# A first stage with one level of Strassen's scheme for gate projections, and the softmax division on ScalarE

## The chip, the cores and the metric

The kernel runs on one core of a Trainium2 chip. The metric is the device time of one execution in microseconds. A core has five engines that run side by side: TensorE (PE, matrix products), VectorE (DVE), ScalarE (ACT), GpSimd (POOL) and SyncE (SP, here only a queue of transfers); transfers run on 16 DMA engines.

## What is computed

One step of a decoder layer for 1024 prompt tokens and 8 sample tokens (1032 columns in all), in float32. Cut to what matters here:

```
h = rms_norm(x) * g                                   # 1032 x 1024
rq, rk, rv, rg, sq, sk, sv, sg, mg_r, mg_s = split(h @ w_in)
o_r = rms_norm(retention(rope(rq), rope(rk), rv)) * silu(rg)      # 4 heads, 1024 columns
o_s = sink_attention(rope(norm(sq)), rope(norm(sk)), sv) * silu(sg)   # 16 heads, window 128
merged = sigmoid(mg_r) * (o_r @ w_br_ret) + sigmoid(mg_s) * (o_s @ w_br_swa)
y = x + merged @ w_out
```

`rg` and `sg` are 1024 columns each (8 column tiles of 128), `mg_r` and `mg_s` together 2048 (16 column tiles). The softmax has one extra "sink" term in its denominator.

## The kernel before

Every large product is made of three matmuls on operands split in a high and a low part (`hi*hi + hi*lo + lo*hi`). The splits are made at run time: ACT rounds a copy (`whi`, line 168), POOL or DVE subtracts it (`wlo`, line 169). `h` lies transposed in SBUF for the whole first phase as `hhi` and `hlo`, 8 slices of 128 rows by 1032 tokens.

A *block* is one column tile of `w_in` times one third of the tokens: `gemm_T` (lines 206 to 214), 8 slices of 128 rows by 3 matmuls with 344 moving columns, 24 matmuls that add up in one PSUM bank. Three kinds of gates are blocks: `ret_q` (retention q, line 302), `gate_block` (a SiLU gate, line 279: tanh on ACT, a product on DVE, a product with the attention's output `oT` on POOL, and after the third block a store to `d_o`), and `mg_block` (merge gate, line 292: tanh on ACT, a store to `d_t` from ACT's queue).

The first phase (`groups`, line 695) goes through 8 groups: 4 retention heads (`ret_tile`, line 342, and `ret_rows`), then 4 groups of windowed attention (`swa_tile`, line 492, and `swa_rows`). Each group has 8 token tiles. A tile begins with `gemm_tok`, 24 matmuls with 384 moving columns, and goes on in three to five later parts, which `groups` places between the parts of the tiles behind it (`pipe`). All blocks are filler between them: `FILL[gi]` merge-gate blocks and the 6 gate blocks of the group before (`prev`) are spread over a group's tiles, `TAIL[gi]` of them kept for its last tile. What is left of the merge gates follows behind the last group, together with the last 6 gate blocks. The order written in `groups` gives priorities; the order of the instructions on each engine is planned from them when the kernel is built, by a model of the time line, so that the parts of several steps lie interleaved in an engine's queue.

Weights come in units (`load_unit`, line 151): one transfer into one of 3 `wraw` buffers on SP's queue, then the split into one of `wbufs = 6` pairs. `run_steps` loads up to `look` units ahead.

The step order at the start is: `norm_h` (line 240) for the 9 token tiles, with the loads of the first head's k and v weights, its q weights and the rotary tables in between; the x tiles borrow buffers of the `oT` and `qT` tiles. `softmax_tail` (line 477) ends with the division as one product on DVE, line 490:

```
        nc.vector.reciprocal(out=r[:p, :nh], in_=l[:p, :nh])
        nc.vector.tensor_tensor(out=s[:p], in0=s[:p], in1=r[:p, :nh].unsqueeze(2).broadcast_to([p, nh, P]), op=ALU.mult)
```

Behind the groups `open_a` (line 838) reads the first 7 tiles of the gated retention output back from `d_o` through the two `oT` buffers and splits them (`opA0` to `opA6`, lines 881 and 882) into memory that the windowed attention used. The second phase (`phase23`, line 890) multiplies by `w_br_ret`, `w_br_swa` and `w_out`.

## Time and profile before

| | |
|---|---|
| median of 3 runs | 1188.82 us (1187.67 to 1190.15) |
| the profiled execution: its time, its span | 1189.96 us, 1188.1 us |
| PE busy, PE weight loads busy | 1166.6 us (98%), 1103.2 us (93%) |
| DVE, ACT, POOL busy | 644.3 us (54%), 438.7 us (37%), 429.0 us (36%) |
| mean granted clock of TensorE | 0.997 of full speed |
| PE's share of the chain that ended last | 92% |
| moved by DMA | 116.61 MB, mean 98 GB/s |

Times in the views are microseconds from the first instruction. The duration that is listed for a matmul is longer than the distance to the next one, since matmuls are pipelined; the distance between two starts tells what one costs.

### The profile page before, as it was taken

Reading aid. Unit: us, or ns where it says so; the run is one execution under the profiler, and the core shown is the slowest. Engines: PE = TensorE matmul, PEld = TensorE weight load, DVE = VectorE, ACT = ScalarE, POOL = GpSimd, SP = SyncE. Lnnn points to the kernel's source line nnn. Section 1 sums busy time; section 2 is a strip of 40 time slices with the busy share of each in tenths; the row PEclk is TensorE's granted clock in tenths of the full one; section 3 lists DMA queues with packets and bytes.
Section 4 is the critical chain, followed back from the end, with each engine's and each line's share of the span. In section 5 each row is a group of like instructions: output and inputs, shape, how many; then the busy total and the mean of one; then the engine's idle time right before and its main releaser. Section 6 shows DMA issues by size and latency. Waiting matters only on the chain.

```text
span 1188.1 us, 19187 instructions
## 1 busy us (share of the span) xinstructions
PE 1166.6 (98%) x7116; PEld 1103.2 (93%) x7116; DVE 644.3 (54%) x1798; ACT 438.7 (37%) x1130; POOL 429.0 (36%) x395
## 2 busy tenths in 40 slices
PE   6999999999999999999999999999999999999998
PEld 5899999999989999999999999999999999999876
DVE  5755545544644386776775677477843411654121
ACT  6533333344234235544463446345544210221010
POOL 5325116215325435533563356235751221221010
PEclk9999999999999999999999999999999999999999
DMA  9224114313123411220141014101537744644221
GB/s 321 59 73 115 60 43 146 113 60 94 49 69 84 136 63 46 74 79 7 59 129 43 10 60 126 47 1 37 174 104 242 232 143 138 187 127 142 74 91 69
DMA packets 125165, 116.61 MB, mean 98 GB/s; under 512 B 17480, under 2 KB 113224, under 8 KB 125040
## 3 DMA queue, kind: packets, MB, share of 16 engines
q1 hardware_dynamic: 118160, 106.93, 29.2%
q10 hardware_dynamic: 6912, 8.46, 2.0%
q8 instruction: 56, 0.92, 0.3%
q14 instruction: 37, 0.30, 0.1%
HBM read 84.98 MB, written 32.44 MB: 99 GB/s over the span
## 4 chain that ended last, share of the span: by engine, by line
PE 92%; DMA 2%; DVE 2%; issue 1%; ACT 1%; POOL 1%; SPq 0%; ACTq 0%; POOLq 0%
PE acc L212 16%; PE acc L213 16%; PE acc L214 16%; PE acc L224 10%; PE acc L223 10%; PE acc L222 10%; PE acc L233 1%; PE acc L232 1%; PE sc L532 1%; PE av L441 1%; PE sc L533 1%; PE av L564 1%; PE av L565 1%; PE tr L544 1%; DMA oT<-d_o 1%
## 5 line engine op out<-in xcount | busy, mean ns | idle before, releaser
L169 POOL TENSOR_TENSOR wlo<-wraw,whi 128x1024 fp32r<-128x1024 f32 (+1 forms) x92 | 206.7, 2253 | 311.7 <-ACT whi L168 268.8
L212 PE MATMUL acc<-hhi,whi 128*128 128x344 f32 x864 | 279.9, 324 | 2.0 <-ACT tg L298 2.0
L214 PE MATMUL acc<-hhi,wlo 128*128 128x344 f32 x864 | 277.5, 322 | 0.0
L213 PE MATMUL acc<-hlo,whi 128*128 128x344 f32 x864 | 277.1, 321 | 0.0
L222 PE MATMUL acc<-whi,hhi 128*128 128x384 f32 x512 | 175.6, 344 | 2.3 <-ACT hhi L139 1.2
L224 PE MATMUL acc<-whi,hlo 128*128 128x384 f32 x512 | 175.3, 342 | 0.0
L223 PE MATMUL acc<-wlo,hhi 128*128 128x384 f32 x512 | 175.3, 343 | 0.0
L212 PEld LDWEIGHTS acc<-hhi,whi 128*128 128x128 f32 x864 | 162.9, 188 | 5.5 <-ACT tg L298 2.6
L213 PEld LDWEIGHTS acc<-hlo,whi 128*128 128x128 f32 x864 | 162.6, 188 | 1.6
L214 PEld LDWEIGHTS acc<-hhi,wlo 128*128 128x128 f32 x864 | 162.6, 188 | 1.6 <-issue 0.4
L168 ACT ACTIVATE whi<-wraw 128x1024 fp32r<-128x1024 f32 (+1 forms) x92 | 90.4, 984 | 177.3 <-PE acc L213 114.3
L147 POOL TENSOR_TENSOR rs<-ms,nhalf 128x1 f32<-128x1 f32 (+3 forms) x81 | 69.4, 858 | 216.7 <-DVE ms L146 192.4
L222 PEld LDWEIGHTS acc<-whi,hhi 128*128 128x128 f32 x512 | 97.5, 191 | 6.1 <-issue 2.5
L224 PEld LDWEIGHTS acc<-whi,hlo 128*128 128x128 f32 x512 | 97.3, 190 | 0.5 <-DVE hlo L140 0.2
L223 PEld LDWEIGHTS acc<-wlo,hhi 128*128 128x128 f32 x512 | 97.4, 190 | 0.4
L288 POOL TENSOR_TENSOR oT<-oT,tg 128x344 f32<-128x344 f32 x48 | 48.3, 1007 | 63.1 <-DVE tg L286 58.6
L486 ACT ACTIVATE s<-sc,ng,rs 128x128 f32<-128x128 f32 x128 | 57.0, 456 | 17.4 <-DVE ng L483 17.3
L224 PE MATMUL acc<-whi,mlo 128*128 128x512 f32 x128 | 50.5, 395 | 0.0
L223 PE MATMUL acc<-wlo,mhi 128*128 128x512 f32 x128 | 50.3, 393 | 0.0
L222 PE MATMUL acc<-whi,mhi 128*128 128x512 f32 x128 | 50.1, 393 | 0.0
L965 DVE TENSOR_TENSOR x<-acc,x 128x512 f32<-128x512 f32 x16 | 11.0, 690 | 68.7 <-PE acc L224 68.7
L286 DVE SCALAR_TENSOR_TENSOR tg<-tg,acc 128x344 f32<-128x344 f32 x48 | 24.5, 511 | 35.7 <-ACT tg L285 35.5
(357 smaller groups left out, 2394.8 us busy)
## 6 DMA issues: line engine op xcount, KB each, us to landing
wraw<-in_w_in SPq DMA_DIRECT2D x36, 512.0 KB
d_t<-tg ACTq DMA_DIRECT2D x48, 172.0 KB
d_o<-oT SPq DMA_DIRECT2D x16, 516.0 KB
tt<-d_t SPq DMA_DIRECT2D x48, 172.0 KB
wraw<-in_w_in SPq DMA_DIRECT2D x32, 256.0 KB
st<-d_o SPq DMA_DIRECT2D x9, 516.0 KB
d_m<-tt SPq DMA_DIRECT2D x24, 172.0 KB
mm<-d_m SPq DMA_DIRECT2D x24, 172.0 KB
```

Source lines behind the costliest of these rows:

```text
L147: nc.gpsimd.tensor_tensor(out=rs[:p, :width], in0=ms[:p, :width], in1=self.nhalf[:p, :width], op=ALU.pow)
L168: nc.scalar.activation(out=hi[:, :f], in_=raw[:, :f], func=AF.Copy)
L169: nc.gpsimd.tensor_tensor(out=lo[:, :f], in0=raw[:, :f], in1=hi[:, :f].bitcast(F32), op=ALU.subtract)
L212: nc.tensor.matmul(ps, whi[:, k, :], hi[:, cs], start=(k == 0), stop=False)
L213: nc.tensor.matmul(ps, whi[:, k, :], lo[:, cs], start=False, stop=False)
L214: nc.tensor.matmul(ps, wlo[:, k, :], hi[:, cs], start=False, stop=(k == KT - 1))
L222: nc.tensor.matmul(ps, hi[:, k, a:b], whi[:, kk, :], start=(k == 0), stop=False)
L223: nc.tensor.matmul(ps, hi[:, k, a:b], wlo[:, kk, :], start=False, stop=False)
L224: nc.tensor.matmul(ps, lo[:, k, a:b], whi[:, kk, :], start=False, stop=(k == KT - 1))
L286: nc.vector.scalar_tensor_tensor(out=tg[:], in0=tg[:], scalar=1.0, in1=ps[:, :BL], op0=ALU.add, op1=ALU.mult)
L288: nc.gpsimd.tensor_tensor(out=sl, in0=sl, in1=tg[:], op=ALU.mult)
L486: nc.scalar.activation(out=s[:p, j, :], in_=src[j], func=AF.Exp, bias=ng[:p, j : j + 1], scale=scale[j], accum_out=l[:p, j : j + 1])
```

## The change

**Strassen's scheme.** A new first stage, `phase0`, stands ahead of the groups. It takes `norm_h` (with buffers of its own), computes the merge gates of the first 4 column tiles as blocks as before, builds sums of parts of `h` on POOL, DVE and ACT (`make_T`, for two quarters q of the tokens), and then computes 3 pairs of merge-gate column tiles and all 8 retention-gate column tiles (4 pairs) in a 2 by 2 split: the 1024 rows of the inner dimension in two halves, the two column tiles, and the tokens in two halves. A pair takes 7 products (`product`) for each of two quarters q: 4 slices of 128 rows by 3 matmuls with 258 moving columns. The weight operands of a pair are made by `load_part`: two loads, four sums on DVE, three and a half splits. ACT and DVE combine the products (`keep`, `put`). Merge gates go to `d_t`, retention gates to a new DRAM tensor `d_g`; later `gate_apply` reads them back and multiplies `oT` by them on POOL where a `gate_block` stood.

**The groups** lose this filler: `FILL` and `TAIL` become shorter, the retention groups keep only their own `ret_q` blocks, and the first head's k, v and q weights and the tables are loaded behind `phase0`.

**The softmax division** becomes four activations on ACT with a scale for each partition.

```
 RAW = 3
 NA1 = 7
-XQ = 4
 XPOOL = (6,)
-QAT = (1, 2, 4)
+HALF = TOK // 2
+QT = HALF // 2
+B11, B21, B22, T1, T3, T4, T2 = range(7)
+FIRST = 4
+PAIRS = 3
 ROW = [2, 0, 0, 0, 2, 0, 0, 1]
-FILL = [3, 2, 2, 2, 9, 9, 9, 4]
-TAIL = [2, 4, 4, 5, 3, 5, 5, 2]
+FILL = [0, 0, 0, 0, 7, 3, 3, 1]
+TAIL = [0, 0, 0, 0, 1, 1, 1, 0]
...
+def pair_units(col):
+    return [("S", col, part) for part in range(4)]
...
+        if spec[0] == "S":
+            return self.load_part(*spec[1:])
...
+    def load_part(self, col, part):
+        nc = self.nc
+        if part == 0:
+            self.praw = []
+            for e in range(2):
+                raw = self.t(self.wp, [P, D], "wraw", bufs=RAW)
+                src = self.i["w_in"][0, :, col + e * P : col + (e + 1) * P].rearrange("(k p) c -> p k c", p=P)
+                nc.sync.dma_start(out=raw[:].rearrange("p (k c) -> p k c", k=KT), in_=src)
+                self.praw.append(raw)
+        one, two = self.praw
+        if part == 1:
+            self.sums = self.t(self.sp, [P, 3, 512], "wsum", bufs=1)
+            s1, s2, s4 = [self.sums[:, k] for k in range(3)]
+            a11, a12, a21, a22 = one[:, 0:512], one[:, 512:1024], two[:, 0:512], two[:, 512:1024]
+            nc.vector.tensor_tensor(out=s1, in0=a21, in1=a22, op=ALU.add)
+            nc.vector.tensor_tensor(out=s2, in0=s1, in1=a11, op=ALU.subtract)
+            nc.vector.tensor_tensor(out=s4, in0=a12, in1=s2, op=ALU.subtract)
+            nc.vector.tensor_tensor(out=a21, in0=a11, in1=a21, op=ALU.subtract)
...
+        if part == 2:
+            self.nsd += 1
+            both = self.sd[:, self.nsd % 2 * 1024 : (self.nsd % 2 + 1) * 1024]
+            hi, lo = both[:, :512], both[:, 512:]
+        else:
+            hi = self.t(self.wp, [P, D], "whi", F32R, bufs=self.wbufs)[:]
+            lo = self.t(self.wp, [P, D], "wlo", F32R, bufs=self.wbufs)[:]
+        nc.scalar.activation(out=hi, in_=src, func=AF.Copy)
+        nc.gpsimd.tensor_tensor(out=lo, in0=src, in1=hi.bitcast(F32), op=ALU.subtract)
+        return hi, lo
...
+        small = lambda u: u[0] == "S" and u[2] == 2
+
+        def room(idx):
+            kind = small(units[len(loaded)])
+            n = sum(1 for j in range(len(loaded)) if last[j] >= idx and small(units[j]) == kind)
+            return n < (2 if kind else self.wbufs)
...
+    def operand(self, q, b, j, x):
+        c = q * QT + (HALF if b == B22 else 0)
+        if b >= T1:
+            return self.T[q][j][x][:, b - T1, :]
+        h = (self.hhi, self.hlo)[x]
+        return h[:, j + (4 if b != B11 else 0), c : c + QT]
+
+    def product(self, ps, part, half, q, b, start=True, stop=True, **kw):
+        nc = self.nc
+        whi, wlo = part
+        for j in range(4):
+            ws = slice(half * 512 + j * P, half * 512 + (j + 1) * P)
+            hi, lo = [self.operand(q, b, j, x) for x in range(2)]
+            nc.tensor.matmul(ps[:, :QT], whi[:, ws], hi, start=(start and j == 0), stop=False, **kw)
+            nc.tensor.matmul(ps[:, :QT], whi[:, ws], lo, start=False, stop=False, **kw)
+            nc.tensor.matmul(ps[:, :QT], wlo[:, ws], hi, start=False, stop=(stop and j == 3), **kw)
+
+    def ring(self):
+        self.ncc += 1
+        return self.cc[:, self.ncc % 4 * HALF : (self.ncc % 4 + 1) * HALF].rearrange("p (h n) -> p h n", h=2)
...
+    def pair_steps(self, col, q, finish):
+        nc = self.nc
...
+        def put(e, half, a, b, op=ALU.add):
+            if e not in v:
+                v[e] = self.ring()
+            nc.vector.tensor_tensor(out=v[e][:, half], in0=a[:, :QT], in1=b, op=op)
+
+        def keep(name, of):
+            v[name] = self.t(self.gp, [P, BL], "tg", bufs=3)[:, :QT]
+            nc.scalar.activation(out=v[name], in_=v[of][:, :QT], func=AF.Copy)
+
+        def p1(us):
+            self.product(acc("X"), us[0], 0, q, B11, True, False, **part)
+            keep("s1", "X")
+
+        def p2(us):
+            self.product(acc("Y"), us[0], 1, q, B21)
+            put(0, 0, v["Y"], v["s1"])
+
+        def p5(us):
+            self.product(acc("Z"), us[0], 0, q, T1, True, False, **part)
+            keep("s5", "Z")
+
+        def p6(us):
+            self.product(v["X"], us[0], 1, q, T2, False, False, **part)
+            keep("s2", "X")
+
+        def p3(us):
+            self.product(v["Z"], us[0], 0, q, B22, False, True, **part)
+            put(0, 1, v["Z"], v["s2"])
+            finish(0, q, v[0])
+
+        def p4(us):
+            self.product(acc("W"), us[0], 1, q, T4)
+            keep("s4", "W")
+
+        def p7(us):
+            self.product(v["X"], us[0], 0, q, T3, False, True, **part)
+            put(1, 1, v["X"], v["s5"])
+            put(1, 0, v["X"], v["s4"], ALU.subtract)
+            finish(1, q, v[1])
+
+        a, m, d, b = pair_units(col)
+        return [([a], p1), ([a], p2), ([m], p5), ([m], p6), ([d], p3), ([b], p4), ([b], p7)]
...
+    def make_T(self, q, pool, scratch):
+        nc = self.nc
+        self.T[q] = []
+        h0 = slice(q * QT, (q + 1) * QT)
+        h1 = slice(HALF + q * QT, HALF + (q + 1) * QT)
+        H, L = self.hhi[:].bitcast(F32), self.hlo[:].bitcast(F32)
+        for j in range(4):
+            r = scratch(j)[:, : 4 * QT].rearrange("p (a n) -> p a n", a=4)
+            left = lambda x: x[:, j::4, h1]
+            right = lambda x: x[:, j].rearrange("p (h n) -> p h n", h=2)[:, :, h0]
+            nc.gpsimd.tensor_tensor(out=r[:, 0:2], in0=left(H), in1=right(H), op=ALU.subtract)
+            nc.gpsimd.tensor_tensor(out=r[:, 2:4], in0=left(L), in1=right(L), op=ALU.subtract)
+            nc.vector.tensor_tensor(out=r[:, 0:2], in0=r[:, 0:2], in1=r[:, 2:4], op=ALU.add)
+            nc.vector.tensor_tensor(out=r[:, 3], in0=H[:, j + 4, h1], in1=r[:, 0], op=ALU.subtract)
+            nc.vector.tensor_tensor(out=r[:, 3], in0=r[:, 3], in1=L[:, j + 4, h1], op=ALU.add)
+            nc.gpsimd.tensor_tensor(out=r[:, 2], in0=r[:, 3], in1=H[:, j + 4, h0], op=ALU.subtract)
+            nc.gpsimd.tensor_tensor(out=r[:, 2], in0=r[:, 2], in1=L[:, j + 4, h0], op=ALU.subtract)
+            hi, lo = [self.t(pool, [P, 4, QT], f"T{q}{j}{x}", F32R) for x in "hl"]
+            nc.scalar.activation(out=hi[:], in_=r, func=AF.Copy)
+            nc.vector.tensor_tensor(out=lo[:], in0=r, in1=hi[:].bitcast(F32), op=ALU.subtract)
+            self.T[q].append((hi, lo))
...
+    def put_quarter(self, dst, src, q):
+        self.nc.scalar.dma_start(out=dst.rearrange("p (h q n) -> p q h n", h=2, q=2)[:, q], in_=src)
+
+    def mg_pair(self, c, q, cc):
+        self.nc.scalar.activation(out=cc, in_=cc, func=AF.Tanh, scale=0.5)
+        self.put_quarter(self.d_t[c], cc, q)
+
+    def gate_pair(self, kt, q, cc):
+        nc = self.nc
+        tg = self.ring()
+        nc.scalar.activation(out=tg, in_=cc, func=AF.Tanh, scale=0.5)
+        nc.vector.scalar_tensor_tensor(out=tg, in0=tg, scalar=1.0, in1=cc, op0=ALU.add, op1=ALU.mult)
+        self.put_quarter(self.d_g[kt], tg, q)
+
+    def gate_apply(self, kt, nb, oT, i):
+        nc = self.nc
+        n0 = nb * BL
+        tg = self.t(self.gp, [P, BL], "tg", bufs=3)
+        nc.sync.dma_start(out=tg[:], in_=self.d_g[kt][:, n0 : n0 + BL])
+        sl = oT[:, i, n0 : n0 + BL]
+        nc.gpsimd.tensor_tensor(out=sl, in0=sl, in1=tg[:], op=ALU.mult)
+        if nb == NB - 1:
+            self.stored = nc.sync.dma_start(out=self.d_o[kt], in_=oT[:, i, :])
+
+    def phase0(self):
+        nc, tc = self.nc, self.tc
...
+        def begin(us):
+            self.sp = enter("sp")
+            ctx["pT0"] = enter("T0"), ctx["T0"]
+            self.xb = enter("xb")
+
+        def t0(us):
+            pool = ctx.pop("pT0")[0]
+            self.make_T(0, pool, lambda j: self.t(self.xb, [P, 4 * QT], "scr", bufs=2))
+
+        def t1(us):
+            leave("xb")
+            pool = enter("T1")
+            raw = [self.t(self.gp, [P, 2, TOK], "oT", bufs=2)[:].rearrange("p a b -> p (a b)") for _ in range(2)]
+            self.make_T(1, pool, lambda j: raw[j % 2][:, j // 2 * 1032 :])
+            self.sd = self.t(self.gp, [P, 2, TOK], "oT", F32R, bufs=2)[:].rearrange("p a b -> p (a b)")
+            self.cc = self.t(self.gp, [P, 2, TOK], "oT", bufs=2)[:].rearrange("p a b -> p (a b)")
+            self.nsd = self.ncc = 0
+
+        def end(us):
+            for name in ("T1", "T0", "sp"):
+                leave(name)
+
+        x = lambda t: ([], lambda us: self.norm_h(t), 0)
+        w = lambda u: ([u], nop, 0)
+        first = [tch(OFF_MR + c * P) for c in range(FIRST)]
+        conv = lambda nb: [([u], (lambda us, c=c, nb=nb: self.mg_block(us[0], c, nb)), 4 if nb == 2 else 0) for c, u in enumerate(first)]
+        steps = [([], begin, 0), x(0), w(first[0]), x(1), w(first[1]), x(2), w(first[2]), x(3), w(first[3])]
+        steps += [x(t) for t in range(4, NT + 1)]
+        steps += conv(0) + [([], t0, 0)] + conv(1) + [([], t1, 0)] + conv(2)
+        jobs = [(OFF_MR + c * P, lambda e, q, cc, c=c: self.mg_pair(c + e, q, cc)) for c in range(FIRST, FIRST + 2 * PAIRS, 2)]
+        jobs += [(OFF_RG + c * P, lambda e, q, cc, c=c: self.gate_pair(c + e, q, cc)) for c in range(0, KT, 2)]
+        for col, fin in jobs:
+            for q in range(2):
+                steps += self.pair_steps(col, q, fin)
+        steps.append(([], end))
+        steps.append(([tch(OFF_RQ)], nop))
+        self.run_steps(steps, 4)
...
         nc = self.nc
         p = P if t < NT else NS
         cs = slice(t * P, t * P + p)
-        if t == XQ:
-            x = self.t(self.ap, [P, TOK], "qT", bufs=2)[:, :D]
-        else:
-            i = t - (t > XQ)
-            if i % 2 == 0:
-                self.xpair = self.t(self.gp, [P, 2, TOK], "oT", bufs=2)
-            x = self.xpair[:, i % 2, :D]
+        x = self.t(self.xb, [P, D], "xt", bufs=4)
         nc.sync.dma_start(out=x[:p], in_=self.i["x_prompt"][0, cs, :] if t < NT else self.i["x_sample"][:, 0, :])
         if t == 0:
-            self.gb = self.t(self.ap, [P, D], "st", bufs=1)
+            self.gb = self.t(self.xb, [P, D], "gb")
...
-        nc.vector.tensor_tensor(out=s[:p], in0=s[:p], in1=r[:p, :nh].unsqueeze(2).broadcast_to([p, nh, P]), op=ALU.mult)
+        for j in range(nh):
+            nc.scalar.activation(out=s[:p, j, :], in_=s[:p, j, :], func=AF.Copy, scale=r[:p, j : j + 1])
...
+            with tc.tile_pool(name="pacc0", bufs=6, space=PSUM, reuse_waits="tile") as self.pacc, \
+                    tc.tile_pool(name="ptr0", bufs=2, space=PSUM, reuse_waits="tile") as self.ptr:
+                self.phase0()
...
-        mg = [([tch(OFF_MR + c * P)], (lambda us, c=c, nb=nb: self.mg_block(us[0], c, nb))) for c in range(16) for nb in range(NB)]
+        mg = [([tch(OFF_MR + c * P)], (lambda us, c=c, nb=nb: self.mg_block(us[0], c, nb))) for c in range(FIRST + 2 * PAIRS, 16) for nb in range(NB)]
...
-                col = (OFF_RG + kt * P) if gi < 4 else (OFF_SG + (kt - 8) * P)
+                col = OFF_SG + (kt - 8) * P
                 for nb in range(NB):
+                    if gi < 4:
+                        yield ([], (lambda us, kt=kt, nb=nb, i=i: self.gate_apply(kt, nb, st["o"], i)))
+                        continue
...
-        x = lambda t: ([], lambda us: self.norm_h(t), 0)
-        w = lambda u: ([u], nop, 0)
-        steps += [([], begin, 0), x(0), w(kv[0]), x(1), w(kv[1]), x(2), w(kv[2]), w(kv[3]), ([], tables, 0), x(3), w(qu),
-                  x(4), x(5), rope_block(0), x(6), x(7), x(8), rope_block(1), rope_block(2)]
+        steps += [([], begin, 0), rope_block(0), ([], tables, 0), rope_block(1), rope_block(2)]
...
-                if h:
-                    put(*qs)
+                put(*qs)
...
-                if gi == 0 and t in QAT:
-                    put(qs[QAT.index(t)])
```

## Rows read from the trace of the kernel before

**Rows 1.** The page, part 1: busy time, share of the span, instructions.
```profile
PE 1166.6 (98%) x7116; PEld 1103.2 (93%) x7116; DVE 644.3 (54%) x1798; ACT 438.7 (37%) x1130; POOL 429.0 (36%) x395
```

**Rows 2.** Stretches of the start: length, busy time of each engine, clock, DMA.
```profile
28.00:32.00 4.00, 4.00 (x17) 4.00 (x17) 3.12 (x16) 3.59 (x9) 0.73 (x2) 0.61 1.14 303
...
sum 60.00, PE 46.47 PEld 42.94 DVE 40.14 ACT 34.33 POOL 27.10; mean PE 3.10 PEld 2.86 DVE 2.68 ACT 2.29 POOL 1.81
```

**Rows 3.** PE's instructions in order of time, the start.
```profile
11.20 0.69 PE L222 MATMUL acc<-whi,hhi 128*128 128x384 f32 x1 [1.19 <-ACT hhi L139]
...
20.51 0.60 PE L271 MATMUL tr<-ident,oT 128*128 128x128 f32 x4
```

**Rows 4.** PE's instructions in order of time: start, duration, line, tile, shapes.
```profile
66.08 0.32 PE L214 MATMUL acc<-hhi,wlo 128*128 128x344 f32 x1
...
67.96 0.32 PE L214 MATMUL acc<-hhi,wlo 128*128 128x344 f32 x1
...
71.46 0.28 PE L202 MATMUL sc<-Shi,qhi 128*128 128x256 f32 x1
...
72.17 0.38 PE L339 MATMUL tr<-ident,on 128*128 128x128 f32 x2
```

**Rows 5.** Groups by line, PE's weight loads: busy, mean ns, idle before.
```profile
L213 PEld LDWEIGHTS acc<-hlo,whi 128*128 128x128 f32 x864 | 162.6, 188 | 1.6
```

**Rows 6.** Stretches of the groups: busy PE, PEld, DVE, ACT, POOL, clock, DMA.
```profile
310.00:360.00 50.00, 50.00 (x309) 45.47 (x309) 26.19 (x95) 20.09 (x60) 10.28 (x14) 1.00 0.19 58
760.00:830.00 70.00, 70.00 (x438) 65.79 (x437) 54.32 (x186) 32.04 (x98) 25.64 (x27) 1.00 0.06 19
421.00:833.00 412.00, 411.84 (x2577) 392.21 (x2576) 288.78 (x940) 192.55 (x571) 188.49 (x182) 1.00 0.18 55
...
833.00:905.00 72.00, 70.57 (x453) 69.29 (x452) 43.70 (x82) 34.52 (x80) 40.59 (x36) 1.00 0.51 164
60.00:390.00 330.00, 330.00 (x2083) 312.95 (x2082) 167.28 (x507) 126.75 (x337) 112.63 (x115) 1.00 0.27 84
```

**Rows 7.** The same stretches, line 212 alone (8 of its matmuls a block).
```profile
310.00:360.00 50.00, 5.39 (x16) 3.00 (x16) 1.00 0.19 58
760.00:830.00 70.00, 18.11 (x56) 10.52 (x56) 1.00 0.06 19
...
833.00:905.00 72.00, 41.01 (x128) 23.93 (x128) 1.00 0.51 164
```

**Rows 8.** Groups by line and shape: the division on DVE.
```profile
L490 DVE TENSOR_TENSOR s<-s,r 128x512 f32<-128x512 f32 x32 | 23.1, 721 | 0.6
```

**Rows 9.** Groups by line and shape: ACT with a scale for each partition.
```profile
L354 ACT ACTIVATE khi<-kr,misc 128x128 fp32r<-128x128 f32 x32 | 12.8, 399 | 16.0 <-DVE kr L322 11.5 <-PE av L203 4.5
```

**Rows 10.** Groups by line and shape: POOL's products and differences.
```profile
L169 POOL TENSOR_TENSOR wlo<-wraw,whi 128x1024 fp32r<-128x1024 f32 x60 | 145.2, 2422 | 284.1 <-ACT whi L168 241.2 <-PE acc L233 42.8
...
L288 POOL TENSOR_TENSOR oT<-oT,tg 128x344 f32<-128x344 f32 x48 | 48.3, 1007 | 63.1 <-DVE tg L286 58.6 <-DVE mx L539 4.0 <-DVE l L488 0.5
```

**Rows 11.** PE and DVE in order of time, from retention to windowed attention.
```profile
396.92 0.39 PE L369 MATMUL av<-qT,kT 128*128 128x128 f32 x2
...
414.31 0.75 DVE L455 TENSOR_TENSOR qr<-acc,Aswa_q_g 128x256 f32<-128x256 f32 x2 [3.03 <-POOL Aswa_q_g L649]
...
417.01 0.44 PE L222 MATMUL acc<-whi,hhi 128*128 128x384 f32 x1 [1.15 <-DVE tg L286]
```

**Rows 12.** DVE in order of time, and the chain of waits, 820 to 925.
```profile
884.08 0.85 DVE L571 TENSOR_TENSOR oT<-av,rbig 64x256 f32<-64x256 f32 x2 [7.90 <-ACT rbig L567]
...
900.40 6.18 DMA oT<-d_o
...
907.80 1.30 DVE opA6l L882
```

More of the change, by code (lines that the diff above doesn't have):

```diff
@@ L186, in run_steps @@
         loaded = [self.loaded[u] for u in pre]
-        def live(idx):
-            return sum(1 for j in range(len(loaded)) if last[j] >= idx)
+        small = lambda u: u[0] == "S" and u[2] == 2
[3 more added lines that the diff above has]
+            return n < (2 if kind else self.wbufs)
         for idx, (us, fn, look) in enumerate(steps):
             top = max([max(n) for n in need[: idx + 1] if n], default=-1)
-            while len(loaded) < len(units) and len(loaded) <= top + look and live(idx) < self.wbufs:
+            while len(loaded) < len(units) and len(loaded) <= top + look and room(idx):
                 loaded.append(self.load_unit(units[len(loaded)]))
@@ L669, in build @@
             self.d_t = [self.t(dp, [P, TOK], f"d_t{k}") for k in range(16)]
+            self.d_g = [self.t(dp, [P, TOK], f"d_g{k}") for k in range(8)]
             self.d_m = [self.t(dp, [P, TOK], f"d_m{k}") for k in range(8)]
@@ L727, in first @@
             return (us, fn), ([], more)
-        kv = slabs([(OFF_RK, DK), (OFF_RV, DV)])
-        qu = tch(OFF_RQ)
         def begin(us):
```

24 lines of the change are left out of this document (23 added, 1 removed).

## The prediction

> **What bounds the kernel now.** I read the page first: PE is busy for 1166.6 of 1188.1 us, and no other engine comes over 54% [rows 1]. A number of PE instructions, times what each costs, is therefore the first measure of this change; the second is whether PE still finds work wherever filler is taken away. For the second I read stretches. In the first 60 us PE loses 13.5 us, and part of the rest runs at half clock (0.61 of full speed in one row, which is a mix of the 1.2 and 2.4 GHz levels) [rows 2]. From 60 to 390 (retention) and from 421 to 833 (windowed attention) it loses 0.0 and 0.2 us; from 833 to 905, where the attention ends and `open_a` reads back, 1.4 us [rows 6]. The reader is to see that filler makes PE full: in the windowed attention DVE is at 70% of the stretch, and from 760 to 830 blocks are 38% of PE's time [rows 6, 7].
>
> **What a block costs, and a product.** The listed durations overlap, so I count starts. Twelve matmuls of 344 columns go from 66.08 to 67.96, 0.1567 us each; six of 256 columns from 71.46 to 72.17, 0.1183 us each [rows 4]. A block is 24 x 0.1567 = 3.76 us. The line through the two gives 0.1192 us for 258 columns. A pair of column tiles was 6 blocks, 144 matmuls, 22.56 us; it becomes 2 x 7 x 12 = 168 matmuls, 20.03 us. That is 2.53 us less, not an eighth, because there are more matmuls and each has a part that does not shrink with its columns. Seven pairs: **-17.7 us**. At the price of 256 columns it would be -18.8.
>
> The price of 168 matmuls at no less than the old pitch is a rival below. It comes from the Trainium skill's page "Perfetto Trace Analysis", section "Identifying the Most-Contended Engine", which judges TensorE's headroom by the busy share of its weight loads and not of its matmuls. By that, loads at 93% [rows 1] would make 24 more weight loads a pair a loss. The trace disagrees so far: a load lasts 188 ns, yet starts of 256-column matmuls, each with a load of its own, lie 118 ns apart [rows 4, 5].
>
> **The start, 0 us.** Transposes of the first tile still wait for x. Before, products began at 11.20; a block needs three token tiles, and the third tile's second half is transposed at 20.51 [rows 3], so about 9 us of half-clock work moves back. In return the tables (five transfers) are no longer on SP's queue among the x tiles, x has four buffers, and the later waits of the 13.5 us find 12 blocks (45 us) that need nothing else. I take 0, between -4 and +4.
>
> **Making the sums of h, +1 us.** Per slice POOL has two operations of 516 elements and two of 258. Between 1.007 us for 344 and 2.422 us for 1024 [rows 10] that is 1.37 and 0.83, so 4.4 us a slice, 35 us for eight. The blocks run from about 20 to 70 us. POOL can begin near 31 us, when the seventh tile is split, is done near 66, and still needs 2.4 us for the first pair's low part. It just fits. Late by a whole quarter's sums it would cost 10: bounds 0 and 10.
>
> **The pairs, +1 us.** In 20 us a pair asks POOL for 3 x 2.4 + 1.2 = 8.5 us and DVE and ACT for about 10 each, so they hide. Between the fifth product and the third, ACT must copy Z out while PE does one product (1.43 us); behind a 1 us weight split it is late. I allow 0.07 us for each of 14 quarters; bounds 0 and 4.
>
> **Into retention, +1 us.** Rotary tables and slabs now load at the end of `phase0`. Three `ret_q` blocks (11.3 us) cover what is late; without them all of it would stall: 0 to 8.
>
> **The thinner retention groups, +1 us.** 27 blocks go (3 + 3 x 8), 102 us of the stage. From 60 to 390, 330 us become some 228 with DVE at 167 at most (73%) and ACT at 127 (56%) [rows 6]. Blocks will be the three `ret_q` in 57 us, 20%. The nearest row is 310 to 360: two blocks (16 matmuls of line 212, 15% of PE) and PE at 50.00 of 50 [rows 6, 7]. So dense, at bounds 0 and 10. `gate_apply` adds 24 loads to SP's queue; each waits for one of three `tg` buffers, that is for POOL's product, and behind it stand weight loads. Three raw buffers and six split pairs loaded ahead hide it; else a unit comes late by the product's 1.0 us [rows 10].
>
> **Into the windowed attention, +2 us.** Between the last retention score at 396.92 and the first rotary product at 414.31 the new group has no tables; PE lives on two gemms and blocks and loses 1.15 us at 417.01 [rows 11]. Then 9 and 6 blocks were at hand; now 7, without gates. Bounds 0 and 10.
>
> **The body, with the division, +1 us.** 8 + 6 + 6 + 3 = 23 blocks go, 86.5 us, so 412 become 325. DVE gives up 32 x 0.721 = 23.1 us [rows 8] and is left with 266 (82%). ACT takes 128 activations; the nearest row, of 128x128 with a scale for each partition, is 0.399 us [rows 9], so 51 us more, 244 at most (75%). Both stay below PE. The nearest row is 760 to 830: seven blocks, 38% of PE, DVE at 78%, PE at 70.00 of 70 [rows 6, 7]. Groups with 9 blocks are like it; the two with 7 are thinner. Chain per tile: 0.72 us becomes up to 4 x 0.40. Bounds 0 and 8.
>
> **The end of the attention, +4 us.** From the last product on `oT` at 884.08 to `opA6` at 909.1 runs a chain of its own, 25 us: gates, store, loads (one takes 6.18 us), splits [rows 12]. From 833 to 905, 128 / 8 = 16 blocks covered it and the last tiles [rows 7]; now 6 gates and 4 merge-gate blocks do, 22.6 us less. DVE is busy for 43.7 of these 72 us [rows 6], so the last tiles can finish earlier once PE is free for them, which gives most back. Bounds 0 and 22.6; I take 4, nearer the lower.
>
> **Sum.** -17.7 + 0 + 1 + 1 + 1 + 1 + 2 + 1 + 4 = -6.7 us on the profiled execution's 1189.96, which lies 1.1 us above the median: 1182 us. The likeliest case reaches from 1176 to 1186. 0.2% (2.4 us) is what a measurement can tell from no change.
>
> **Rivals.**
> Dense everywhere: the planner packs the thinner stages as well as before (for it: zero idle at 15% filler; against it: PE already slips where filler is short, 833 to 905). The small terms fall to 2: 1189.96 - 1.1 - 15.7 = 1173. Chance 0.27.
> The tail starves, slower than before: the last tiles take as long as now and the chain into `opA6` finds no block left. The full 22.6 us stand for the 4: 1201. It decides from 11 us of idle there. For it: that chain is already the last to end. Against it: DVE's slack. Chance 0.20.
> DVE and ACT become the bound in the thin attention groups: at half of the upper ends, entry and body cost 9 us in place of 3, 1188, no gain. For it: 82% and 75%. Against it: 78% beside a full PE. Chance 0.10.
> Weight loads bind, so that Strassen doesn't do what it says: 168 x 0.1567 = 26.3 us a pair, +3.8 each, +26 for -17.7: 1226. Against it the 118 ns. Chance 0.03.
> The forecast has 0.40. Faster: 0.38 + 0.27 + 0.02 = 0.67; same 0.11; slower 0.22. The range takes in the dense case with the start's gain (1168) and almost all of the tail's case: 1168 to 1199.
>
> **What would show it.** Starts 0.119 us apart in the pairs, a pair in 20 us. PE without waits from 25 to 65, and no wait for POOL where the first product on sums begins. PE idle under 1 us in each retention group. In the attention groups waits of PE on DVE or ACT of a few us. Behind the last tile, waits on `opA` splits of 5 to 7 us. I am wrong if the pitch is above 0.125 (the pairs' gain is gone at 0.134), if PE waits for over 10 us behind the last tile, or if retention shows 10 us of idle.

## The result and the profile after

The changed kernel takes 1257.89 us (median of 4, 1256.78 to 1260.19) beside 1188.24 of the kernel before on the same chip: a ratio of 1.0586, 95% interval 1.0566 to 1.0607. It is slower by 69.7 us, where 6.7 us of gain were forecast; the range ended at 1199.

The page after, part 1, as [rows 1]:

```profile
PE 1175.2 (94%) x7284; PEld 1096.2 (87%) x7284; DVE 718.6 (57%) x1870; ACT 510.2 (41%) x1326; POOL 489.4 (39%) x441
```

PE's idle time grew from 21.5 us (1188.1 less 1166.6) to 79.9 (1255.1 less 1175.2). Its busy time grew by 8.6 us although the products became 17.7 us cheaper, and the mean granted clock fell from 0.997 to 0.979. The granted clock was 0.50, the lower level of 1.2 GHz, for 52 us in all. PE was busy for 33.3 of them and idle for the others (the sum over these stretches):

```profile
sum 51.99, PE 33.34 PEld 29.08 DVE 35.60 ACT 20.32 POOL 24.77; mean PE 4.17 PEld 3.64 DVE 4.45 ACT 2.54 POOL 3.10
```

So half of 33.3, 16.7 us of PE's busy time, is lost to the clock, against 3.4 before; what else is lost at the lower level is idle time and counted there. Where PE loses its time, the stretches after tell (length, busy time of each engine with its instructions, clock, DMA), in the form of [rows 2, 6]:

```profile
0.00:60.00 60.00, 41.76 (x254) 39.42 (x255) 37.35 (x49) 31.14 (x54) 34.08 (x31) 1.00 0.56 169
60.00:120.00 60.00, 48.90 (x325) 47.40 (x324) 39.32 (x45) 22.78 (x37) 44.94 (x32) 0.83 0.19 62
120.00:240.00 120.00, 120.00 (x994) 119.83 (x993) 51.07 (x80) 51.28 (x93) 52.30 (x27) 1.00 0.37 115
240.00:510.00 270.00, 266.78 (x1661) 247.13 (x1660) 176.39 (x534) 111.46 (x326) 97.53 (x111) 1.00 0.33 105
510.00:540.00 30.00, 18.61 (x106) 16.08 (x105) 12.54 (x54) 6.14 (x19) 16.68 (x21) 0.79 0.47 148
540.00:930.00 390.00, 361.19 (x2151) 331.90 (x2150) 286.82 (x912) 215.24 (x674) 176.51 (x183) 0.98 0.17 51
930.00:990.00 60.00, 56.55 (x344) 53.88 (x343) 27.63 (x56) 32.28 (x74) 22.77 (x22) 0.97 0.35 119
```

The pairs (120 to 240) and retention (240 to 510) are full, as forecast. Three places are not: the making of the sums (60 to 120), the entry to windowed attention (510 to 540) and its body (540 to 930). With the idle time, and half of the time in which PE was busy at the lower clock (5.6, 2.3 and 7.1 us), they lose 17, 14 and 36 us.

**The pairs.** These two starts are 15 matmuls apart: 0.1193 us each, so a pair of 168 matmuls takes 20.0 us, as predicted.

```profile
179.96 0.28 PE L279 MATMUL acc<-T03h,whi 128*128 128x258 f32 x1
...
181.75 0.28 PE L279 MATMUL acc<-hhi,oT 128*128 128x258 f32 x1
```

**The sums of h.** POOL's instructions in order of time (start, duration, in brackets the idle time before and what ended it):

```profile
48.21 2.56 POOL L349 TENSOR_TENSOR scr<-hhi 128x516 f32<-128x516 f32 x2 [6.15 <-ACT hhi L146]
...
59.34 6.93 POOL L349 TENSOR_TENSOR oT<-hhi 128x516 f32<-128x516 f32 x4 [0.18 <-ACT hhi L146]
66.22 1.32 POOL L349 TENSOR_TENSOR scr<-hhi 128x516 f32<-128x516 f32 x1
...
90.47 0.64 POOL L354 TENSOR_TENSOR scr<-scr,hhi 128x258 f32<-128x258 f32 x1 [0.89 <-DVE scr L353]
```

It begins at 48, not 31, and the second quarter's sums (`oT`) run ahead of the first quarter's third and fourth slice (`scr`), which are done only past 90. PE waits for them (its longest wait from 60 to 120: total, times, longest). During the wait its clock falls to the lower level, and it stays there while PE works in pieces:

```profile
PE acc L279 <- ACT T02h L357: 7.9, 1, 7.9
```

```profile
84.00:88.00 4.00, 1.01 (x9) 0.81 (x7) 3.96 (x7) 0.00 (x0) 2.54 (x3) 0.86 0.00 0
88.00:92.00 4.00, 0.00 (x0) 0.00 (x0) 2.26 (x4) 0.17 (x1) 2.69 (x5) 0.50 0.00 0
92.00:96.00 4.00, 2.67 (x9) 2.08 (x9) 1.23 (x1) 0.91 (x2) 3.95 (x5) 0.50 0.00 0
...
104.00:108.00 4.00, 4.00 (x22) 4.00 (x22) 3.49 (x7) 2.67 (x4) 1.17 (x2) 0.58 0.01 4
```

**The entry.** POOL stands on `gate_apply` (line 381), whose loads are late, before it makes the attention's tables (lines 864 to 867); PE's first rotary transpose waits 11.16 us. In [rows 11] the longest wait of PE is 1.15, before another instruction:

```profile
519.68 1.81 POOL L381 TENSOR_TENSOR oT<-oT,tg 128x344 f32<-128x344 f32 x2 [5.72 <-DMA tg<-d_g]
...
533.26 0.78 POOL L866 TENSOR_TENSOR Bswa_q_g<-s,gbn 128x288 f32<-128x288 f32 x1
```

```profile
535.22 0.66 PE L727 MATMUL tr<-ident,qr 128*128 128x128 f32 x2 [11.16 <-DVE qr L684]
```

**The body.** These are the longest waits from 540 to 930, by engine. PE's are many and short: 19.4 of 28.8 us for an accumulator, 7.5 for the probabilities that POOL masks. The longest of ACT and DVE are for each other:

```profile
PE acc L443 <- DVE tg L501: 6.9, 5, 2.2
PE acc L262 <- DVE tg L501: 5.5, 4, 2.2
PE av L781 <- POOL pLp L769: 3.8, 4, 1.6
PE av L780 <- POOL pHp L769: 3.4, 3, 2.0
```

```profile
ACT s L701 <- DVE ng L698: 35.9, 17, 4.3
ACT qs L732 <- DVE qs L733: 30.7, 22, 2.9
```

```profile
DVE l L703 <- ACT ds L702: 27.7, 20, 2.2
```

Such waits alone are no sign of loss. Over the whole stage of the windowed attention, from the first rotary transpose to the last product with v, DVE's longest wait in total is the same before, when PE was full, and after:

```profile
DVE l L488 <- ACT ds L487: 32.0, 22, 2.8
```

```profile
DVE l L703 <- ACT ds L702: 32.1, 23, 2.2
```

DVE is busy for 74% of the stretch from 540 to 930 and ACT for 55%. Neither is full, and yet the stage is shorter by much less than the blocks that it lost. From the first rotary transpose to the last product with v (535.22 to 968.41; before 421.34 to 882.86), first the whole row, and under it line 262 (before 212) alone, 8 of whose matmuls make a block:

```profile
535.22:968.41 433.19, 403.12 (x2400) 369.91 (x2400) 307.12 (x981) 238.71 (x742) 196.03 (x203) 0.98 0.18 53
...
535.22:968.41 433.19, 106.91 (x320) 62.33 (x320) 0.98 0.18 53
```

The same two of before:

```profile
421.34:882.86 461.52, 459.93 (x2886) 439.10 (x2885) 321.44 (x1011) 216.89 (x636) 221.44 (x214) 1.00 0.21 62
...
421.34:882.86 461.52, 155.94 (x482) 90.64 (x482) 1.00 0.21 62
```

60.25 blocks became 40: 20.25 x 3.76 = 76 us of PE's work left the stage, which got only 28.3 us shorter. It lost 48 us.

### The profile page after: what moved, and what is told of

Its sections match the earlier page's. It is cut to its first block, busy times and chain, and to the rows that moved or that the text cites. A ratio compares the mean times of both kernels' runs of the same rounds, so it can differ in the third digit from the quotient of the medians.

```text
span 1255.1 us, 20010 instructions
## 1 busy us (share of the span) xinstructions
PE 1175.2 (94%) x7284; PEld 1096.2 (87%) x7284; DVE 718.6 (57%) x1870; ACT 510.2 (41%) x1326; POOL 489.4 (39%) x441
## 5 line engine op out<-in xcount | busy, mean ns | idle before, releaser
L178 POOL TENSOR_TENSOR wlo<-wraw,whi 128x1024 fp32r<-128x1024 f32 (+1 forms) x78 | 171.2, 2203 | 248.2 <-ACT whi L177 166.4
L262 PE MATMUL acc<-hhi,whi 128*128 128x344 f32 x528 | 174.1, 332 | 9.2 <-DVE tg L501 6.2
L264 PE MATMUL acc<-hhi,wlo 128*128 128x344 f32 x528 | 172.4, 327 | 0.0
L263 PE MATMUL acc<-hlo,whi 128*128 128x344 f32 x528 | 172.3, 326 | 0.0
L177 ACT ACTIVATE whi<-wraw 128x1024 fp32r<-128x1024 f32 (+1 forms) x78 | 75.2, 969 | 114.0 <-PE acc L453 43.6
L262 PEld LDWEIGHTS acc<-hhi,whi 128*128 128x128 f32 x528 | 101.8, 193 | 12.8 <-DVE tg L501 7.5
L263 PEld LDWEIGHTS acc<-hlo,whi 128*128 128x128 f32 x528 | 101.6, 192 | 0.8
L264 PEld LDWEIGHTS acc<-hhi,wlo 128*128 128x128 f32 x528 | 101.3, 192 | 0.6
L299 DVE TENSOR_TENSOR oT<-acc,tg 128x258 f32<-128x258 f32 x56 | 22.4, 421 | 59.7 <-PE acc L281 57.3
L215 POOL TENSOR_TENSOR wlo<-wraw,whi 128x1024 fp32r<-128x1024 f32 x14 | 36.0, 2574 | 38.0 <-ACT whi L214 38.0
```

The costliest lines, as they stand in the source:

```text
L177: nc.scalar.activation(out=hi[:, :f], in_=raw[:, :f], func=AF.Copy)
L178: nc.gpsimd.tensor_tensor(out=lo[:, :f], in0=raw[:, :f], in1=hi[:, :f].bitcast(F32), op=ALU.subtract)
L215: nc.gpsimd.tensor_tensor(out=lo, in0=src, in1=hi.bitcast(F32), op=ALU.subtract)
L262: nc.tensor.matmul(ps, whi[:, k, :], hi[:, cs], start=(k == 0), stop=False)
L263: nc.tensor.matmul(ps, whi[:, k, :], lo[:, cs], start=False, stop=False)
L264: nc.tensor.matmul(ps, wlo[:, k, :], hi[:, cs], start=False, stop=(k == KT - 1))
```

## Experiments

Three theories stand at the start. A, thin filler: the blocks that went to the new stage were PE's cover for the attention's chains. B: the division on ACT lengthens these chains. C: the new stage costs more than its products save.

The kernel before ran beside each group of runs; its median lies between 1187.98 and 1189.17 us. A difference between runs of different groups is therefore good to 1 or 2 us.

### Which part of the change costs the time

**The division back on VectorE**, in the changed kernel:

```
-        for j in range(nh):
-            nc.scalar.activation(out=s[:p, j, :], in_=s[:p, j, :], func=AF.Copy, scale=r[:p, j : j + 1])
+        nc.vector.tensor_tensor(out=s[:p], in0=s[:p], in1=r[:p, :nh].unsqueeze(2).broadcast_to([p, nh, P]), op=ALU.mult)
```

> The changed kernel with one part undone: the softmax division is again one VectorE instruction per tile. Three theories. A, thin filler: the merge-gate blocks that went to the new stage were TensorE's cover for the chains of the windowed attention; without them it waits. B, the division: four ScalarE activations behind the reciprocal lengthen each tile's chain and hold up ScalarE's queue. C, the new stage itself: the sums of h and what stands around them cost what the products save and more. A and C: the division is a small part, 1245 to 1262 us. B: the attention's loss goes, 1225 us or less.

1248.15 us, ratio to before 1.0489 (1.0471 to 1.0507): by the medians the division is 9.7 of the 69.7 us, by the ratios 11.5.

**The division alone**, the reverse edit in the kernel before.

> The kernel before with the softmax division alone moved to ScalarE. A and C: with all its filler the attention hides the longer chain, 1184 to 1196 us. B: 1210 us or more.

1194.94 us, 1.0042 (1.0030 to 1.0054): 5.8 us with all the filler. B is a part and not the main cause.

**Plain blocks in the pairs' place**, no sums:

```
-        for col, fin in jobs:
-            for q in range(2):
-                steps += self.pair_steps(col, q, fin)
+        steps += [([tch(OFF_MR + c * P)], lambda us, c=c, nb=nb: self.mg_block(us[0], c, nb)) for c in range(FIRST, FIRST + 2 * PAIRS) for nb in range(NB)]
+        steps += [([tch(OFF_RG + c * P)], lambda us, c=c, nb=nb: self.gate_early(us[0], c, nb)) for c in range(KT) for nb in range(NB)]
```

> The changed kernel with the seven pairs computed by 42 plain blocks at the same place ahead of retention, and no sums of h or of weights. The order of everything behind the stage is the same. A: the products cost 17.7 us more, the sums' stall of about 15 us goes, the attention is as thin as in the changed kernel: about 1260 us, 1245 to 1272. C: the loss goes with the sums, 1215 us or less.

1254.31 us, 1.0540 (1.0521 to 1.0559). Without any Strassen product the loss is the same but for 3.6 us: it lies in what was moved, and in the division, which this run keeps. The stage as built costs as much as its products save.

**The filler given back**:

```
-PAIRS = 3
-FILL = [0, 0, 0, 0, 7, 3, 3, 1]
-TAIL = [0, 0, 0, 0, 1, 1, 1, 0]
+PAIRS = 0
+FILL = [0, 0, 0, 0, 10, 9, 9, 4]
+TAIL = [0, 0, 0, 0, 3, 5, 5, 2]
```

> The changed kernel with pairs for the retention gates alone (four in place of seven); the six merge-gate columns of the other three pairs are plain blocks again and stand in the attention groups, 10, 9, 9 and 4 merge-gate blocks with 4 left behind the last group, held back as before the change. A: three pairs' gain is lost (+7.6), some 25 to 35 of the attention's 41 us come back and most of the 12 at its entry: about 1222 us, 1210 to 1238. B and C: nothing comes back, 1258 to 1270.

1225.83 us, 1.0301 (1.0282 to 1.0320): 32 us faster with three pairs' gain given up. The body is dense again (4.6 us idle in its whole stage); the wait at the entry is still 11.6 us.

**The kernel before, thinned**: nothing but merge-gate blocks moved to retention, 23 from the attention groups and 2 from behind them (the 18 of the expectation are miscounted; in the stage, blocks fall from 60.3 to 40.8). The blocks kept for each last tile become as few as in the changed kernel.

```
-FILL = [3, 2, 2, 2, 9, 9, 9, 4]
-TAIL = [2, 4, 4, 5, 3, 5, 5, 2]
+FILL = [8, 8, 8, 10, 1, 3, 3, 1]
+TAIL = [2, 4, 4, 5, 1, 1, 1, 0]
```

> The kernel before with nothing changed but where its plain blocks stand: 18 merge-gate blocks of the attention groups go to the retention groups (8, 8, 8, 10 and 1, 3, 3, 1), held back as in the changed kernel, so that each attention group has as many blocks as there. No sums, no pairs, the division on VectorE. If thin filler alone makes the attention wait, 1218 to 1242 us. If the new stage or the division were needed for it: 1195 us or less.

1240.90 us, 1.0444 (1.0429 to 1.0460). The same 7116 instructions on PE, in another order, cost 52 us more. A is shown, in the kernel before, with no part of the change in it. 19.5 blocks, 73 us, left the stage, which got 25.5 us shorter (436.0 for 461.5): 48 us lost, as in the changed kernel. Part 1 of its page:

```profile
PE 1184.5 (95%) x7116; PEld 1112.7 (90%) x7116; DVE 675.7 (54%) x1798; ACT 434.9 (35%) x1130; POOL 428.5 (35%) x395
```

Against [rows 1], 34.9 us of idle time and 17.9 us of busy time are added. Of the latter 12.6 are the clock (0.985 for 0.997 on the mean): PE was busy for 32 us at 0.50, before for 6.8.

### The sums of h and the entry

The first four start from the kernel with the filler given back (1225.83 us).

**Gate products later at the entry**: `k = 8 if gi == 4 else 2` blocks stand ahead of `prev` in a group.

> The kernel of the run with the filler given back (four pairs, 1225.8 us), and in the first attention group the six gate products on GpSimd go behind eight merge-gate blocks in place of two. That run still waits 11.6 us where the first rotary product needs the attention's tables: GpSimd stands on the gate products, whose loads are late, ahead of the tables it has to make, and TensorE has no block to do. If that order is the cause, 8 to 12 us come back: 1213 to 1219 us. Rival: the tables' loads behind the change of pools are late by themselves: 1223 to 1228 us.

1225.03 us. The time is in the rival's range, but not for the rival's reason: the wait falls from 11.6 to 5.4 us, so the order does matter there. PE's idle time falls by 3.1 us in all (57.5 to 54.4) and the time hardly; in the rest of the stage PE idles 3.4 us more. That blocks used at the entry are missing later would explain it, and was not tried by itself.

**Four scratch slices**: `make_T(0, ...)` gets the two `oT` tiles that `make_T(1, ...)` uses behind it.

> The same kernel of 1225.8 us, and the sums of the first quarter get four scratch slices (the two oT tiles that the second quarter uses behind them) in place of a ring of two, so that GpSimd no longer turns to the second quarter before the first is done. If the ring of two is what makes the first quarter late, 8 to 14 of the 16 us that the stage loses come back: 1211 to 1218 us. Rival: GpSimd's rate, and its contention with VectorE, set the time whatever the order: 1221 to 1227 us.

1220.90 us, 4.9 less by the medians and 3.2 by the ratios, where 8 to 14 were put down to the ring. PE now waits 10.2 us there for ACT's split of a pair's weights.

**All sums on VectorE**, on top of it: each `nc.gpsimd` in `make_T` becomes `nc.vector`.

> As the run with four scratch slices, and all sums of h on VectorE, none on GpSimd. If rate and contention matter (a 516-element sum takes 0.68 us on VectorE alone, 1.8 to 2.9 beside GpSimd's), it is 3 to 10 us faster than that run; if the order alone matters, it is within 3 us of it.

1211.51 us, 1.0196 (1.0179 to 1.0214): 9.4 less again, so rate and contention are the larger part; PE's idle time from 60 to 120 falls from 11.4 us to 2.6. The sum of 516 elements on DVE (line 351; behind the bar the busy time in us and the mean ns of one) after, and then in this run:

```profile
L351 DVE TENSOR_TENSOR oT<-oT 128x516 f32<-128x516 f32 x4 | 7.7, 1918 | 0.0
L351 DVE TENSOR_TENSOR scr<-scr 128x516 f32<-128x516 f32 x4 | 4.9, 1228 | 8.8 <-POOL scr L350 8.8
```

```profile
L351 DVE TENSOR_TENSOR oT<-oT 128x516 f32<-128x516 f32 x8 | 5.3, 685 | 0.0
```

It takes 1.2 and 1.9 us on the mean beside POOL's work and 0.69 without it. POOL's own of 516 take 1.30 us where DVE is idle and up to 2.4 beside it.

**Three mends together** (entry, scratch, division).

> Three mends together on the kernel of 1225.8 us: gate products behind eight blocks at the entry, four scratch slices, and the softmax division on VectorE again. If each part adds up (10, 11 and 5 to 10 us): 1193 to 1202 us. If the causes overlap: 1203 to 1212 us.

1224.69 us, above both ranges, and 3.8 more than with the scratch slices alone: they don't add up. The entry's change or the division must take back what the others give; the two weren't separated here. The gate products are left where they were in the runs that follow.

**Three pairs**: the kernel of 1211.51 us with the last retention head's gates as six plain blocks at the head of the first attention group again (`gates` yields `gate_apply` for `gi < 3`, pairs run over `range(0, 6, 2)`).

> The kernel with four pairs and all sums of h on VectorE (1211.5 us), with three pairs in place of four: the gates of the last retention head are six plain blocks again, at the head of the first attention group, where they stood before the change. If the 11.2 us that TensorE still waits at the entry are missing filler: 2.5 us of products are lost and about 11 come back, 1200 to 1206 us. If they are the tables' own lateness: 1212 to 1217 us.

1204.38 us, 1.0135 (1.0120 to 1.0150). It is 7.1 us faster, so six blocks there are worth 9.6 us (7.1, and 2.5 of the lost pair); 5.4 us of wait remain.

**The division on VectorE, on this.**

> The run with three pairs, and the softmax division on VectorE again. The division cost 9.7 us in the changed kernel and 5 in the kernel before: 4 to 9 us faster than that run, 1192 to 1201 us.

1203.51 us: 0.9 less, where 4 to 9 were expected. With the filler in place the division costs next to nothing here, 5.8 us in the kernel before, and 9.7 us where filler is thin.

**The changed kernel mended**: seven pairs, sums on VectorE with four slices, division on VectorE, thin filler kept.

> The changed kernel with all seven pairs and its own thin filler, but with what the other runs mended: all sums of h on VectorE with four scratch slices (14.3 us with four pairs) and the division on VectorE (9.7 us). If the parts add up: 1234 us, 1228 to 1240; what is left above the kernel before, some 45 us, and the 17.7 us that the pairs save are then what the missing filler costs.

1235.35 us, 1.0397 (1.0371 to 1.0423): the two parts add up. 46.4 us above the 1188.92 of before and the 17.7 of the pairs, 64 us, are left for the missing filler, entry and body.

### Why the attention waits while no engine is full

On the changed kernel (1257.89 us) where nothing else is said.

**ScalarE gives the accumulator back**: `gate_block` copies `ps` to SBUF on ACT, and tanh and the product on DVE read the copy.

> The changed kernel; in a gate block ScalarE copies the accumulator to SBUF and tanh and VectorE read the copy, so that ScalarE alone gives the accumulator back (24 copies more on ScalarE). The longest named waits in the attention are TensorE's for an accumulator that VectorE's gate product still reads (6.9 and 5.5 us). If VectorE's queue in front of that product is the cause, 6 to 15 us come back: 1243 to 1252 us. If the accumulators are only where the wait shows: 1254 to 1262 us.

1262.22 us. The wait for DVE's `tg` is gone from the list, and others stand in its place, for an accumulator too; PE's idle time in the stage is 32.7 us, 30.1 without the edit. The accumulator looks like the place where the wait shows. The 24 copies are more work for ACT, so a small gain could hide behind them.

**Blocks held back**: `TAIL = [0, 0, 0, 0, 3, 5, 5, 2]`.

> The changed kernel with the same number of blocks in each attention group, held back for its last tile as before the change (3, 5, 5, 2 in place of 1, 1, 1, 0). If the number of blocks decides: 1252 to 1264 us. If their place does: 1245 us or less, or over 1270.

1282.59 us, 24.7 more with the same number of blocks. The place decides too. PE's idle time in the stage grows by only 9.8 us (39.9 for 30.1); another 19 are PE's work at the lower clock, 28.5 us lost for 9.3.

**One tile deeper**, and the same on the mended kernel (1235.35 us):

```
-                    put(p1, p2, p1, *f[:1])
-                    put(p2, *f[1:])
+                    put(p1, p3, p2, p1, *f)
```

> The changed kernel with the attention's pipeline one tile deeper: the last part of a tile (its product with v) is issued a step later, behind the next tile's products, so that transposed probabilities have a whole step to be masked and split. The number of blocks and all work stay the same. If the length of a tile's chain against too little work between its links is the cause, 15 to 30 us come back: 1228 to 1243 us. If VectorE's or ScalarE's throughput is: 1250 us or more.

> The mended kernel with seven pairs (1235.4 us) and the deeper pipeline. If the causes add up: 1205 to 1220 us. If the deeper pipeline brings nothing: 1230 to 1240 us.

1260.31 and 1234.66 us: nothing. Room behind the last part is not what is short. By the expectation this speaks for the load of DVE or ACT and against the length of a tile's chain; the rows below take this up.

**No merge-gate blocks in the attention**: `FILL = [4, 4, 3, 3, 0, 0, 0, 0]`.

> The changed kernel with its 14 merge-gate blocks of the attention groups (52.6 us of TensorE) moved into the retention groups; 18 gate blocks stay. If the attention has a length of its own, near 420 us, that its chains set, it hardly gets shorter (433 us from the first rotary transpose to the last product with v now) and the moved blocks are paid in full elsewhere: 1285 to 1310 us. If it is TensorE's work and waits in proportion, the stage gets shorter by as much as it loses: 1254 to 1270 us.

1281.17 us, 23.3 more, between the two ranges and nearer the upper. 12 blocks less, 45.1 us, make the stage 17.4 us shorter (415.8 for 433.2). So it does not have the fixed length that I had put as one case; some 40% of a block's time comes back.

**A shorter chain**, on the mended kernel (in part):

```
-            nc.vector.tensor_reduce(out=mx[:, 2 * i : 2 * i + 2], in_=cur, axis=AX.X, op=ALU.max)
...
-        nc.vector.tensor_tensor(out=mx[:], in0=mx[:], in1=rs[:, 0:G], op=ALU.mult)
...
+        if mx is None:
+            ng = nsink
```

> The mended kernel with seven pairs (1235.4 us), and the softmax of the prompt's tiles without its maximum: the exponent is shifted by the sink alone, so two reductions, the scaling, the choice and the difference on VectorE (some 50 us in the attention) and one exponential on ScalarE leave each tile's chain. If the chain on VectorE and ScalarE sets the stage's length, 25 to 50 us come back: 1185 to 1210 us. If the missing filler costs the same whatever the chain: 1225 to 1236 us.

1196.36 us, 1.0053 (1.0033 to 1.0073): 39 us less, with no block added. The run leaves out the maximum, so nothing in it guards the exponent against large scores; it tells of time and is no version to keep. Each tile's chain loses five instructions on DVE and one on ACT. The stage's row, under it that of the mended kernel:

```profile
522.75:907.64 384.89, 381.49 (x2354) 356.78 (x2355) 278.66 (x857) 195.32 (x575) 198.79 (x202) 0.99 0.19 57
...
520.90:941.96 421.06, 395.80 (x2392) 366.51 (x2393) 330.97 (x1017) 196.68 (x608) 199.19 (x202) 0.98 0.18 54
```

PE is full again (3.4 us idle) with 38 blocks. The stage in nine kernels, from rows of this kind:

| kernel | us | blocks | PE idle | DVE busy | ACT busy |
|---|---|---|---|---|---|
| before | 461.5 | 60.3 | 1.6 | 70% | 47% |
| four pairs, filler back | 454.8 | 56.4 | 4.6 | 65% | 55% |
| before, thinned | 436.0 | 40.8 | 31.6 | 78% | 46% |
| changed | 433.2 | 40.0 | 30.1 | 71% | 55% |
| changed, division on DVE | 422.0 | 39.5 | 25.6 | 78% | 47% |
| changed, held back | 457.6 | 39.3 | 39.9 | 66% | 52% |
| changed, no merge-gate blocks | 415.8 | 28.0 | 49.9 | 71% | 56% |
| mended | 421.1 | 39.8 | 25.3 | 79% | 47% |
| mended, no maximum | 384.9 | 38.1 | 3.4 | 72% | 51% |

The rows near 40 blocks speak against the load of either engine alone. With the division on DVE, DVE does 23 us more (330 for 307 us in the stage) and the stage is 11 us *shorter*: DVE's load alone isn't the bound. From the mended kernel to the one without the maximum ACT's load stays the same (196.7 and 195.3 us), and the stage is 36 us shorter: ACT's load alone isn't it either. The division on ACT adds 42 us to ACT's load, and its four instructions (0.392 us each) make a tile's chain longer, 1.6 us against one of 0.72. What sorts the rows best is both engines' busy time added up: it is 124 to 127% of the stage in the five thin kernels, and 117, 120 and 123% in the three where PE is nearly full. The held-back kernel, with 118%, doesn't fit; only the place of its blocks differs. This is a pattern in nine rows, and 123 and 124 lie close. Whether it is the two engines' load together or the length of a tile's chain through both, the runs don't separate.

No version with pairs beats the kernel before; the nearest is this last one, 0.5% behind it.

## Why the prediction was wrong, point by point

By its own steps, in us. "Measured" is the idle time of the stretch and half of PE's busy time at the lower clock, less the same of before; the pairs go by their pitch.

| step | predicted | measured |
|---|---|---|
| seven pairs | -17.7 | pitch 0.1193, 20.0 a pair: -17.7 |
| start | 0 (-4 to 4) | +1 (18.2, before 13.5 + 3.4) |
| sums of h | +1 (0 to 10) | +17 (11.1 + 5.6) |
| the pairs' own waits | +1 (0 to 4) | 0 |
| retention, entry and groups | +2 (0 to 18) | +3 |
| into the attention | +2 (0 to 10) | +12 (11.4 + 2.3, before 1.8 from 390 to 421) |
| body, with the division | +1 (0 to 8) | +36 (28.8 + 7.1, before 0.2) |
| end | +4 (0 to 22.6) | +4 (3.4 + 1.7, before 1.4) |

The sum, +55, leaves 12 of the 67 us by which the span grew. They lie in PE's busy time: without the clock it is 13 us longer than the old one less 17.7. An estimate from the trace places some 9 of them: PE has 54 waits for 11 before, and the matmul in front of a wait is listed as busy for about 0.2 us longer than the distance to a next start would be. Most of that is the body's too, which by its length lost 48 us and not 36.

**Right:** the products' price; the division's on ACT (0.392 us for 0.399); the retention groups, which stay nearly full with three blocks each; the end, where the loads behind the last tile now show (the chain of waits after, as [rows 12]) but cost what was forecast, though PE waits 2.4 us for the `opA` splits and not 5 to 7. None of the three signs of being wrong came up: the pitch is 0.1193, the waits behind the last tile are 2.4 us, retention idles 3.2. The prediction had set no such sign for the attention's body, where it failed. The rule that weight loads measure TensorE's headroom (the Trainium skill's page "Perfetto Trace Analysis", section "Identifying the Most-Contended Engine"), a rival here, would have made each pair dearer; the trace disagrees, at 0.1193 us a start.

```profile
968.41 0.52 PE av L781
...
974.54 4.93 DMA oT<-d_o
```

**The step that failed by most is the body:** "Both stay below PE. The nearest row is 760 to 830: seven blocks, 38% of PE, DVE at 78%, PE at 70.00 of 70 [...] Groups with 9 blocks are like it". Two things are wrong in it. A dense stretch with seven blocks says only that blocks then stood where they were wanted: the stage as a whole had 60.3 blocks in 461.5 us, 9.1 in 70, and got 40 in 433, 6.5 in 70. And busy shares were taken for room: DVE at 71% of the stage goes with 30 us of waiting on PE, and at 72% with 3. DVE and ACT work in turn on one tile (maximum, exponent, sum, reciprocal, division), and POOL masks behind them. That their shares leave no room because of these turns fits the rows and is argued, not shown: the two engines wait for each other in the kernel before as well. Shown is that blocks which leave the stage don't shorten it by their time, and that taking instructions out of each tile does shorten it. The rival "DVE and ACT become the bound" named the place but went by shares, and gave it 9 us with the entry. The same page and section calls the busy share of VectorE and ScalarE a fair measure of how near their limit they are; in this stage that share doesn't tell whether PE waits, as the 71% and 72% show.

**The entry** failed by the same step ("now 7, without gates"): the blocks counted were not there to be done. All three accumulators were held by tiles whose tables were late, and the tables stood behind `gate_apply` on POOL. Six plain blocks gave 9.6 us back.

**The sums of h** failed on two figures: "POOL can begin near 31 us, when the seventh tile is split, is done near 66". The seventh tile is split only at 48, and POOL begins there. DVE's queue had a pair's sums of weights between the x tiles (27.3 to 34.0), and the transposes of the last x tiles stand 5 us apart among PE's blocks (at 41.9, 46.9 and 51.9); which of the two costs more was not tried. Then DVE and POOL slow each other. The price of POOL's own sums (1.37 and 0.83 us a piece estimated) was near: 1.34 to 1.76 and 0.72 to 0.95 on the mean. Put on VectorE alone, with four slices, the stage gave 14.3 us back.

**A term was missing altogether:** the clock. After its waits PE works on at the lower level for a while, and of the 67 us 13 are this (16.7, before 3.4). I had priced waits by their own length.

What stays open: whether the chain's length or the load of DVE and ACT together holds the stage, and which link is the first to be late, since the shorter chain was made by taking out six instructions at once; and whether the 14 merge-gate blocks could be placed so that seven pairs pay.

## What to carry to other kernels

Work that looks like idle filler has a price in the stage that it leaves: here only some 40% of a block's time came back from the attention. Before filler is moved, count blocks per tile over the whole stage, and don't read the busy share of an engine that works in turn with another as room. To try it costs one line: thin the filler of the old kernel and change nothing else (52 us were lost so, where the whole change lost 70). If a stage must live with less filler, shorten its chain first: six small instructions less a tile were worth 39 us.

## What was not expected of the hardware

A wait costs more than its length: in the thinned kernel 34.9 us of added idle time came with 17.9 us of added busy time for the same instructions, 12.6 of them by the clock. Seen closely, in the changed kernel PE's granted clock was 0.50, the lower level, from 88 to 104 us, in a wait and while PE worked in pieces behind it, and it rose behind a stretch in which PE worked without a gap.

DVE's sums of two SBUF operands take 1.8 to 2.8 times as long on the mean beside POOL's work (0.69 us to 1.2 and 1.9). The Trainium skill's page "SBUF — State Buffer", section "SBUF: two separate sides", says that VectorE, with two SBUF inputs, and GpSimd take turns on a port pair, one instruction at a time; the trace agrees as far as these sums go. In the attention the sum of the rotary parts (line 684, before 469) went from 0.461 to 0.857 us on the mean, with a longest of 2.63. The trace says where: 21 of the 32 take 0.40 to 0.54 us, and the 11 that take 0.72 to 2.63 all run beside a subtraction of POOL that makes a `wlo` (line 178), as only 3 of the others do; before, 2 of 32 were slow, one of them beside a `wlo`. These 11 add 14 us to DVE's busy time in the stage. What they cost the kernel was not tried.
